# Up projection of a hybrid decoder layer: one PSUM bank per 128-column tile, other uses of the spare banks, and a later place for the query and key transposes

## Chip, cores and metric

The kernel runs on one core of one Trainium2 chip. The metric is device time in microseconds, the median of several executions. The profile is of one execution of the same program.

## The reference

One decoder layer for 256 tokens of width 2048, everything in float32: two attention mixers (8 heads each) on one combined projection, merged by two gates; a squared-ReLU MLP; a gated input embedding.

```python
h = rmsnorm(x, g_mix)
qa, ka, va, qb, kb, vb, ga, gb = split(h @ w_in)              # 2048 x 10240
qa, ka = partial_rope(rmsnorm(qa, qn_gain)), partial_rope(rmsnorm(ka, kn_gain))
ya = dilated_mixture(qa, ka, va)
yb = stick_breaking(qb, kb, vb)
merged = sigmoid(ga) * (ya @ w_branch_a) + sigmoid(gb) * (yb @ w_branch_b)
x = x + merged @ w_out
x = x + square(relu(rmsnorm(x, g_mlp) @ w_up)) @ w_down       # 2048 x 8192, 8192 x 2048
x = x + (p @ w_ple_proj) * sigmoid(rmsnorm(x, g_ple) @ w_ple_gate)
```

## The kernel before

**Number format.** Every weight and activation is split into a high and a low half (`split`, lines 79 to 87: ACT writes the high half on L82, or L85 with a gain; DVE the low half on L83 or L86). A product is three products: high by high, high by low, low by high. A weight load is 1 MB into one of three `raw` buffers (`load`, L91, on SP's queue); `split_weights` cuts it into splits of 1024 columns a row, `wh` and `wl`, three buffers each.

**Order.** The program is written in one order per engine, and a scheduler of the framework, which knows each engine's work and buffers, may draw instructions forward when it lays out the queues. Each engine then works its queue in that order. Steps that should come some time after what they depend on are put off by hand: `later(us, fn)` keeps a step until `advance` has counted that many microseconds of planned matmul time.

**Query and key.** `group_m` (lines 145 to 158) multiplies 16 contraction tiles, 1.3 us of planned time each, into two banks, one for each half of the tokens. `qk_norm` (lines 267 to 288) normalises the heads on ACT and DVE; POOL applies the gain and the rotation (lines 279 to 287). `later(22, qk_transpose, ...)` on L288 puts off four transposes into one bank (L293) and a copy on ACT (L294). The normalised tile `qn` lives in a ring of seven buffers until then.

**MLP.** After the out projection `h2` is made by `turn` (lines 468 to 479): transposes L476 and splits L85, L86, put off by 3 us after each column block. The hidden width of 8192 goes in eight slabs of 1024. `up_units(s)` (lines 555 to 574) makes slab `s` in four groups of two 128-column tiles. A group takes both banks of the tag `mm`; for each of 16 contraction tiles and each column tile `j` there is a pair of matmuls, L565 (512 columns: high weights by both halves of `h2`) and L566 (256 columns: low weights by the high half). `hidden` (lines 529 to 551) then adds the two halves of each bank (ACT copies one on L537, DVE adds on L538, in `hs`), takes relu and square and splits the result `u`.

The down projection of slab `s` runs beside the up projection of slab `s + 1`: `together` interleaves the streams. One column block in two goes by `fast_units`, a seven-product scheme in the four banks of the tag `s`. The other goes by `plain_units` (lines 656 to 676), which takes two banks of the tag `m` for each half block `j`: 48 matmuls on L666 to L668, then two additions into the residual `xr` (L461). The eight banks are thus `mm` 2, `s` 4, `m` 2. The up projection of slab 0 has nothing beside it. The last slab goes by `plain_units` alone, beside the small embedding product. The gate (lines 756 to 768) alternates between `m` and `mm`.

Of the kernel before, what the change touches and what calls it, by code (L numbers as in the profile page):

```python
# [9 lines left out]
F32 = mybir.dt.float32  # L10
F32R = mybir.dt.float32r
AF = mybir.ActivationFunctionType
ALU = mybir.AluOpType
# [3 lines left out]
P = 128  # L17
T = 256
D = 2048
DT = D // P  # L20
# [39 lines left out]
def layer_kernel(ctx: ExitStack, tc: tile.TileContext, xt, xm, pt, gains, qkg, cst,  # L60
                 wa, wb, wba, wbb, wo, wup, wdn, wpg, wpp, out):
    nc = tc.nc
# [43 lines left out]
    def weights(src, nk, cols):  # L106
        return split_weights(load(src, nk, cols), nk, cols)
# [4 lines left out]
    def later(us, fn, *args):  # L112

        pending.append((clock[0] + us, len(pending), fn, args))

    def advance(us):
        clock[0] += us
        while True:
            due = [e for e in pending if e[0] <= clock[0]]
            if not due:  # L120
                return
            e = min(due, key=lambda e: e[:2])
            pending.remove(e)
            e[2](*e[3])

    def flat(a):
        return a.rearrange("p a t -> p (a t)")
# [139 lines left out]
    def qk_norm(ps, tt, g, gain, dst):  # L267
        raw = work.tile([P, 4, DH], F32, tag="w2", name="qraw", bufs=W2)
        sq = work.tile([P, 4, DH], F32, tag="w2", name="qsq", bufs=W2)
        nc.scalar.activation(raw.rearrange("p h d -> p (h d)"), ps, AF.Copy, scale=rt[:, tt:tt + 1])  # L270
        nc.vector.tensor_tensor(sq, raw, raw, op=ALU.mult)
        v = work.tile([P, 4], F32, tag="qv", name="qv")
        r = work.tile([P, 4], F32, tag="qr", name="qr")
        nc.vector.tensor_reduce(v, sq, axis=AX.X, op=ALU.add)
        nc.vector.tensor_scalar(v, v, 1.0 / DH, EPS, op0=ALU.mult, op1=ALU.add)
        rsqrt(r, v, 4)
        qn = work.tile([P, 4, DH], F32, tag="w2", name="qn", bufs=W2)
        nc.vector.tensor_tensor(qn, raw, r[:, :, None].to_broadcast([P, 4, DH]), op=ALU.mult)
        nc.gpsimd.tensor_tensor(qn, qn, gain[:, None, :].to_broadcast([P, 4, DH]), op=ALU.mult)
        ro = work.tile([P, 4, 4, HALF], F32, tag="ro", name="ro", bufs=1)  # L280
        x1, x2 = qn[:, :, :HALF], qn[:, :, HALF:ROT]
        cos = cs[:, C_COS + tt * HALF:C_COS + (tt + 1) * HALF][:, None, :].to_broadcast([P, 4, HALF])
        sin = cs[:, C_SIN + tt * HALF:C_SIN + (tt + 1) * HALF][:, None, :].to_broadcast([P, 4, HALF])
        for n, (a, b) in enumerate(((x1, cos), (x2, sin), (x2, cos), (x1, sin))):
            nc.gpsimd.tensor_tensor(ro[:, n], a, b, op=ALU.mult)
        nc.gpsimd.tensor_tensor(x1, ro[:, 0], ro[:, 1], op=ALU.subtract)
        nc.gpsimd.tensor_tensor(x2, ro[:, 2], ro[:, 3], op=ALU.add)
        later(22, qk_transpose, qn, tt, g, dst)  # L288

    def qk_transpose(qn, tt, g, dst):  # L290
        tp = bank("at")
# [6 lines left out]
    for n, (dst, gain) in enumerate(((qT, gq[:, 0, :]), (kT, gq[:, 1, :]))):  # L298
        for g in range(2):
            if rt is None:  # L300
                ps = group_m(range(4), h, first_weights)
# [4 lines left out]
            else:  # L306
                ps = group_m([wa[2 * n + g, c] for c in range(4)], h)
# [91 lines left out]
    for n, dst in enumerate((qS, kS)):  # L399
        for g in range(4):  # L400
            later(2, dilated_head, 4 * n + g)
            ps = group_t([wb[4 * n + g, c] for c in range(2)], h)
# [17 lines left out]
    for g in range(8):  # L420
        later(2, sb_head, g)
        ps = group_t([wb[8 + g, c] for c in range(2)], h)
        for j in range(2):
            nc.vector.tensor_tensor(gs(2 * g + j), halves(ps[j]), rb, op=ALU.mult)
    for g in range(8):
        ps = group_t([wba[g, 0]], ya)
        for j in range(2):
            k = 2 * g + j
# [4 lines left out]
    m = new_acts("m")  # L433
    for g in range(8):
        pg = group_t([wb[16 + g, c] for c in range(2)], h)
        sg = []
        for j in range(2):
            s = work.tile([P, T], F32, tag="w1", name="sg", bufs=W1)
# [3 lines left out]
        ps = group_t([wbb[g, 0]], yb)  # L442
        for j in range(2):
            k = 2 * g + j
# [52 lines left out]
    h2 = new_acts("h2_", pool=blk)  # L497
    ss1 = const.tile([P, 2, 4], F32, name="ss1")
    for g in range(4):
        ps = group_m([wo[g, c] for c in range(4)], m)  # L500
# [19 lines left out]
    mw = mlp.enter_context(tc.tile_pool(name="mw", bufs=2))  # L520
# [3 lines left out]
    def bank2(tag, bufs=1):  # L524
        return ps2.tile([P, 512], F32, tag=tag, name=f"ps_{tag}", bufs=bufs)

    turn_bank[0] = lambda: bank2("s", 4)

    def hidden(ps, fast):

        n = 8 if fast else 4
        s = mw.tile([P, 2, T], F32, tag="hs", name="hs", bufs=2)
        for j in range(2):
            t = mw.tile([P, T], F32, tag="ev", name="ev", bufs=2)
            nc.scalar.activation(t, ps[j][:, T:], AF.Copy)  # L537
            nc.vector.tensor_tensor(s[:, j, :], ps[j][:, :T], t, op=ALU.add)  # L538
        nc.scalar.activation(s, s, AF.Relu)
        r = mw.tile([P, n, P], F32, tag="hr", name="hr", bufs=1)  # L540
        nc.scalar.activation(r[:, 0:4, :].rearrange("p a t -> p (a t)"),
                             s.rearrange("p a t -> p (a t)"), AF.Square)
        if fast:
            a21, a11, a22, a12 = (r[:, i, :] for i in range(4))
            nc.vector.tensor_tensor(r[:, 4, :], a11, a21, op=ALU.subtract)
            nc.vector.tensor_tensor(r[:, 5, :], a21, a22, op=ALU.subtract)
            nc.vector.tensor_tensor(r[:, 6, :], r[:, 5, :], a11, op=ALU.subtract)
            nc.vector.tensor_tensor(r[:, 7, :], r[:, 6, :], a12, op=ALU.add)
        u = hid.tile([P, 2, n, P], F32R, tag="hid", name="u")
        split(u[:, 0], u[:, 1], r)  # L550
        return u

    A21, A11, A22, A12, S3, S1, S2, S4 = range(8)

    def up_units(s, out):

        for g in range(4):
            ps = [bank2("mm", 2) for _ in range(2)]
            for c in range(2):
                parts = weights(wup[4 * s + g, c], 8, 256)  # L560
                for i, (wh, wl) in enumerate(parts):
                    kt = 8 * c + i
                    for j in range(2):
                        cc = slice(j * P, (j + 1) * P)
                        nc.tensor.matmul(ps[j], wh[:, cc], flat(h2[kt]), start=kt == 0, stop=False)  # L565
                        nc.tensor.matmul(ps[j][:, :T], wl[:, cc], h2[kt][:, 0, :], start=False,  # L566
                                         stop=kt == DT - 1)
                    advance(0.69)
                    if i == 3:
                        yield  # L570
                if c == 0:
                    yield
            out.append(hidden(ps, (s, 0) in FAST or (s, 1) in FAST))
            yield

    def fast_units(s, n, f):

# [78 lines left out]
    def plain_units(s, n, u):  # L656

        for j in range(2):
            ps = [bank2("m", 2) for _ in range(2)]
            for i in range(2):  # L660
                raw = load(wdn[s, n, i, j], 4, PIECE)
                for k, (wh, wl) in enumerate(split_weights(raw, 4, PIECE)):
                    for tt in range(2):
                        a = 2 * i + tt
                        last = i == 1 and k == 3
                        nc.tensor.matmul(ps[tt], u[k][:, 0, a, :], wh, start=i + k == 0, stop=False)  # L666
                        nc.tensor.matmul(ps[tt], u[k][:, 0, a, :], wl, start=False, stop=False)  # L667
                        nc.tensor.matmul(ps[tt], u[k][:, 1, a, :], wh, start=False, stop=last)  # L668
                    advance(1.36)
                    if k == 1:  # L670
                        yield
                if i == 0:
                    yield
            for tt in range(2):
                add_rows(tt, (2 * n + j) * PIECE, ps[tt], r2[:, tt:tt + 1])
            yield
# [52 lines left out]
            finished(2 * n + 1)  # L729

    hids = [[]]
    for _ in up_units(0, hids[0]):
        pass
    for s in range(7):
        hids.append([])
# [18 lines left out]
        nc.sync.dma_start(out[tt, :, c], o)  # L754

    for g in range(4):
        ps = [bank2(("m", "mm")[g % 2], 2) for _ in range(2)]
        for c in range(4):
            for i, (wh, wl) in enumerate(weights(wpg[g, c], 4, PIECE)):
                kt = 4 * c + i  # L760
                for tt in range(2):
                    t = slice(tt * P, (tt + 1) * P)
                    nc.tensor.matmul(ps[tt], h3[kt][:, 0, t], wh, start=kt == 0, stop=False)
                    nc.tensor.matmul(ps[tt], h3[kt][:, 0, t], wl, start=False, stop=False)
                    nc.tensor.matmul(ps[tt], h3[kt][:, 1, t], wh, start=False, stop=kt == DT - 1)
                advance(1.36)
        for tt in range(2):
            gate_out(g, tt, ps[tt], 0, PIECE)
# [3 lines left out]
def tiles_t(w, nk=8):  # L772

    k, n = w.shape
    w = w.reshape(k // (P * nk), nk, P, n // 256, 256).transpose(3, 0, 2, 1, 4)
    return np.ascontiguousarray(w).reshape(n // 256, k // (P * nk), P, nk * 256)
# [9 lines left out]
def tiles_up(w):  # L786

    k, n = w.shape
    w = w.reshape(k, n // 1024, 2, 4, P).transpose(0, 1, 3, 2, 4).reshape(k, n)
    return tiles_t(np.ascontiguousarray(w))  # L790


def quarters(w):
# [50 lines left out]
```

## Time and profile before

| what | us |
|---|---|
| median of 3 runs | 1508.91 (1507.36 to 1509.26) |
| the profiled execution, whole time | 1509.95 |
| its span, first to last instruction | 1508.2 |
| PE busy | 1477.5 (98%) |
| DVE busy | 1067.6 (71%) |
| ACT busy | 857.8 (57%) |
| POOL busy | 57.3 (4%) |

PE runs the matmuls, DVE is the vector engine, ACT the scalar engine, POOL the general engine, SP the queue that issues the loads. The span lies 1.8 us inside the profiled execution's whole time. A matmul's row is longer than its step: its end is modelled and overlaps the next one's start. A wait in brackets at a row is idle time of that engine just before it, and what ended it.

### The profile page before, as it was taken

The page shows a single profiled execution, that of the slowest core. Times are in us where ns is not written, and L with a number is a line of the kernel's source. Part 1 is how long each engine was busy: PE and PEld are TensorE (multiplying, and loading weights), DVE is VectorE, ACT ScalarE, POOL GpSimd, SP SyncE. Part 2 cuts the span into 40 slices and gives each one's busy share as a digit, 9 for nine tenths or more (in the row PEclk, how much of TensorE's full clock was granted, in tenths as well). Part 3 has the DMA queues.
Part 4 walks back from the last instruction along what each step waited for, and adds up shares of the span by engine and source line. Part 5 has one row for each costly group of instructions (what it writes and reads, how often), then busy time and mean ns, then how long its engine had stood idle before and what let it go on. Part 6 is the DMA issues. An engine that isn't in the chain of part 4 may idle for free.

```text
span 1508.2 us, 19034 instructions
## 1 busy us (share of the span) xinstructions
PE 1477.5 (98%) x7412; PEld 1228.9 (81%) x7412; DVE 1067.6 (71%) x1366; ACT 857.8 (57%) x1153; POOL 57.3 (4%) x75
## 2 busy tenths in 40 slices
PE   8999999999999999999999999999999999999998
PEld 5788888888888888888787887878878787878886
DVE  7875666466676676556778879788787878765554
ACT  6454554489845554555555656556565655655543
POOL 3532000000000000000000000000000000000000
PEclk9999999999999999999999999999999999999999
DMA  7555444544455555457355463644636455444563
GB/s 297 206 189 196 168 168 168 187 174 153 161 191 178 185 196 184 179 203 272 122 207 198 153 242 113 246 172 174 217 141 240 149 199 193 157 149 147 198 222 111
DMA packets 40554, 279.16 MB, mean 185 GB/s; under 512 B 4624, under 2 KB 5136, under 8 KB 7312
## 3 DMA queue, kind: packets, MB, share of 16 engines
q1 hardware_dynamic: 40320, 277.92, 51.4%
q8 instruction: 58, 0.95, 0.3%
q14 instruction: 32, 0.26, 0.1%
q10 hardware_dynamic: 144, 0.02, 0.0%
HBM read 275.83 MB, written 2.10 MB: 184 GB/s over the span
## 4 chain that ended last, share of the span: by engine, by line
PE 90%; DVE 5%; ACT 2%; issue 2%; DMA 0%; POOL 0%; SPq 0%; DVEq 0%; ACTq 0%; POOLq 0%
PE ps_mm L138 16%; PE ps_mm L565 15%; PE ps_mm L139 8%; PE ps_mm L566 8%; PE ps_mm L154 5%; PE ps_mm L155 5%; PE ps_mm L153 5%; PE ps_m L667 4%; PE ps_m L668 4%; PE ps_m L666 4%; PE ps_s L584 3%; PE ps_s L586 3%; PE ps_s L588 2%; DVE wl L83 2%; ACT wh L82 2%
## 5 line engine op out<-in xcount | busy, mean ns | idle before, releaser
L83 DVE TENSOR_TENSOR wl<-raw,wh 128x1024 fp32r<-128x1024 f32 (+1 forms) x462 | 566.0, 1231 | 262.5 <-ACT wh L82 257.2
L82 ACT ACTIVATE wh<-raw 128x1024 fp32r<-128x1024 f32 (+1 forms) x462 | 485.4, 1053 | 353.6 <-PE ps_mm L155 112.4
L565 PE MATMUL ps_mm<-h,wh 128*128 128x512 f32 x1024 | 365.9, 399 | 9.1 <-DVE hs L538 6.1
L566 PE MATMUL ps_mm<-h,wl 128*128 128x256 f32 x1024 | 282.9, 281 | 0.6
L138 PE MATMUL ps_mm<-h,wh 128*128 128x512 f32 x768 | 276.8, 403 | 0.0
L565 PEld LDWEIGHTS ps_mm<-h,wh 128*128 128x128 f32 x1024 | 191.4, 188 | 58.8 <-DVE hs L538 11.1
L139 PE MATMUL ps_mm<-h,wl 128*128 128x256 f32 x768 | 215.4, 280 | 0.0
L566 PEld LDWEIGHTS ps_mm<-h,wl 128*128 128x128 f32 x1024 | 192.8, 189 | 9.3 <-DVE wl L83 2.9
L83 DVE TENSOR_TENSOR wl<-quart,wh 128x1024 fp32r<-128x1024 f32 x98 | 119.9, 1224 | 75.4 <-ACT wh L82 74.7
L138 PEld LDWEIGHTS ps_mm<-h,wh 128*128 128x128 f32 x768 | 144.4, 188 | 33.9
L82 ACT ACTIVATE wh<-quart 128x1024 fp32r<-128x1024 f32 x98 | 103.7, 1058 | 95.0 <-PE ps_mm L565 56.8
L139 PEld LDWEIGHTS ps_mm<-h,wl 128*128 128x128 f32 x768 | 145.1, 189 | 0.3
L667 PE MATMUL ps_m<-wl,u 128*128 128x512 f32 x288 | 113.3, 394 | 2.7 <-DVE wl L83 2.7
L666 PE MATMUL ps_m<-wh,u 128*128 128x512 f32 x288 | 111.2, 392 | 2.5 <-DVE xr L461 2.5
L668 PE MATMUL ps_m<-wh,u 128*128 128x512 f32 x288 | 112.5, 391 | 0.0
L153 PE MATMUL ps_mm<-wh,h 128*128 128x512 f32 x256 | 101.4, 399 | 2.7 <-ACT wh L82 2.7
L154 PE MATMUL ps_mm<-wl,h 128*128 128x512 f32 x256 | 101.3, 396 | 2.4 <-DVE wl L83 2.4
L155 PE MATMUL ps_mm<-wh,h 128*128 128x512 f32 x256 | 100.9, 394 | 0.0
L586 PE MATMUL ps_s<-wl,u 128*128 128x512 f32 x196 | 80.3, 410 | 0.0
L584 PE MATMUL ps_s<-wh,u 128*128 128x512 f32 x196 | 79.5, 405 | 0.7 <-ACT wh L82 0.7
L588 PE MATMUL ps_s<-wh,u 128*128 128x512 f32 x196 | 76.7, 392 | 0.0
L667 PEld LDWEIGHTS ps_m<-wl,u 128*128 128x128 f32 x288 | 54.1, 188 | 15.9 <-DVE wl L83 5.3
(210 smaller groups left out, 1989.5 us busy)
## 6 DMA issues: line engine op xcount, KB each, us to landing
raw<-in_wup SPq DMA_DIRECT2D x64, 1024.0 KB, 4.8
raw<-in_wb SPq DMA_DIRECT2D x48, 1024.0 KB, 4.8
raw<-in_wdn SPq DMA_DIRECT2D x36, 1024.0 KB, 4.7
raw<-in_wa SPq DMA_DIRECT2D x31, 1024.0 KB, 4.8
quart<-in_wdn SPq DMA_DIRECT2D x28, 1024.0 KB, 4.7
raw<-in_wo SPq DMA_DIRECT2D x16, 1024.0 KB, 4.8
raw<-in_wpg SPq DMA_DIRECT2D x16, 1024.0 KB, 4.8
raw<-in_wba SPq DMA_DIRECT2D x8, 1024.0 KB, 4.7
```

Source lines behind the costliest of these rows:

```text
L82: nc.scalar.activation(hi, src, AF.Copy)
L83: nc.vector.tensor_tensor(lo, src, hi.bitcast(F32), op=ALU.subtract)
L138: nc.tensor.matmul(ps[j], wh[:, c], flat(rhs[kt]), start=kt == 0, stop=False)
L139: nc.tensor.matmul(ps[j][:, :T], wl[:, c], rhs[kt][:, 0, :], start=False, stop=kt == last)
L153: nc.tensor.matmul(ps[tt], lhs[kt][:, 0, t], wh, start=kt == 0, stop=False)
L154: nc.tensor.matmul(ps[tt], lhs[kt][:, 0, t], wl, start=False, stop=False)
L155: nc.tensor.matmul(ps[tt], lhs[kt][:, 1, t], wh, start=False, stop=kt == last)
L565: nc.tensor.matmul(ps[j], wh[:, cc], flat(h2[kt]), start=kt == 0, stop=False)
L566: nc.tensor.matmul(ps[j][:, :T], wl[:, cc], h2[kt][:, 0, :], start=False, stop=kt == DT - 1)
L666: nc.tensor.matmul(ps[tt], u[k][:, 0, a, :], wh, start=i + k == 0, stop=False)
L667: nc.tensor.matmul(ps[tt], u[k][:, 0, a, :], wl, start=False, stop=False)
L668: nc.tensor.matmul(ps[tt], u[k][:, 1, a, :], wh, start=False, stop=last)
```

## The change

1. `up_units` goes through the two tiles of a group one after the other. Each tile takes one bank, loads its own 1 MB (16 contraction tiles of 128 columns; the host lays `w_up` out for that) and is added up (ACT copy, DVE addition) at its own end. `hidden` gets the sums. The planned time of a pair is counted singly.
2. Slab 0 takes its banks from the tag `s` (four banks) in place of `mm`.
3. In the last slab the second half of each block takes two banks of `s` in place of `m`.
4. The gate alternates between `s` and `m`.
5. The query and key transposes are emitted 32 us of planned time after their group, not 22.

```diff
-        later(22, qk_transpose, qn, tt, g, dst)
+        later(32, qk_transpose, qn, tt, g, dst)
...
-    def hidden(ps, fast):
+    def hidden(s, fast):
         n = 8 if fast else 4
-        s = mw.tile([P, 2, T], F32, tag="hs", name="hs", bufs=2)
-        for j in range(2):
-            t = mw.tile([P, T], F32, tag="ev", name="ev", bufs=2)
-            nc.scalar.activation(t, ps[j][:, T:], AF.Copy)
-            nc.vector.tensor_tensor(s[:, j, :], ps[j][:, :T], t, op=ALU.add)
         nc.scalar.activation(s, s, AF.Relu)
...
-    def up_units(s, out):
+    def up_units(s, out, tag="mm"):
         for g in range(4):
-            ps = [bank2("mm", 2) for _ in range(2)]
-            for c in range(2):
-                parts = weights(wup[4 * s + g, c], 8, 256)
-                for i, (wh, wl) in enumerate(parts):
-                    kt = 8 * c + i
-                    for j in range(2):
-                        cc = slice(j * P, (j + 1) * P)
-                        nc.tensor.matmul(ps[j], wh[:, cc], flat(h2[kt]), start=kt == 0, stop=False)
-                        nc.tensor.matmul(ps[j][:, :T], wl[:, cc], h2[kt][:, 0, :], start=False,
-                                         stop=kt == DT - 1)
-                    advance(0.69)
-                    if i == 3:
+            sums = mw.tile([P, 2, T], F32, tag="hs", name="hs", bufs=2)
+            for j in range(2):
+                ps = bank2(tag, 4 if tag == "s" else 2)
+                parts = split_weights(load(wup[4 * s + g, j], DT, P), DT, P)
+                for kt, (wh, wl) in enumerate(parts):
+                    nc.tensor.matmul(ps, wh, flat(h2[kt]), start=kt == 0, stop=False)
+                    nc.tensor.matmul(ps[:, :T], wl, h2[kt][:, 0, :], start=False, stop=kt == DT - 1)
+                    advance(0.347)
+                    if kt == 7:
                         yield
-                if c == 0:
-                    yield
-            out.append(hidden(ps, (s, 0) in FAST or (s, 1) in FAST))
-            yield
+                t = mw.tile([P, T], F32, tag="ev", name="ev", bufs=2)
+                nc.scalar.activation(t, ps[:, T:], AF.Copy)
+                nc.vector.tensor_tensor(sums[:, j, :], ps[:, :T], t, op=ALU.add)
+                if j == 1:
+                    out.append(hidden(sums, (s, 0) in FAST or (s, 1) in FAST))
+                yield
...
         for j in range(2):
-            ps = [bank2("m", 2) for _ in range(2)]
+            ps = [bank2("s", 4) if j and s == 7 else bank2("m", 2) for _ in range(2)]
...
-    for _ in up_units(0, hids[0]):
+    for _ in up_units(0, hids[0], "s"):
...
-        ps = [bank2(("m", "mm")[g % 2], 2) for _ in range(2)]
+        ps = [bank2("m", 2) if g % 2 else bank2("s", 4) for _ in range(2)]
```

## Rows read from the trace of the kernel before

**Rows 1.** The page: busy time of each engine; engines in the chain that ended last.
```profile
PE 1477.5 (98%) x7412; PEld 1228.9 (81%) x7412; DVE 1067.6 (71%) x1366; ACT 857.8 (57%) x1153; POOL 57.3 (4%) x75
...
PE 90%; DVE 5%; ACT 2%; issue 2%; DMA 0%; POOL 0%; SPq 0%; DVEq 0%; ACTq 0%; POOLq 0%
```

**Rows 2.** Waits of PE: who waited for whom, total us, times, longest.
```profile
PE ps_mm L565 <- DVE hs L538: 6.1, 11, 0.6
...
PE ps_at L293 <- POOL qn L287: 2.7, 1, 2.7
PE ps_m L667 <- DVE wl L83: 2.7, 6, 0.5
PE ps_m L666 <- DVE xr L461: 2.5, 3, 1.6
...
PE ps_mm L565 <- DVE xr L459: 1.0, 1, 1.0
```

**Rows 3.** Timeline, end of slab 0: start, duration, engine, operation [idle before <- releaser].
```profile
723.12 0.38 ACT L537 ACTIVATE ev<-ps_mm 128x256 f32<-128x256 f32 x1 [1.53 <-PE ps_mm L566]
723.15 0.28 PE L566 MATMUL ps_mm<-h,wl 128*128 128x256 f32 x1
...
723.53 0.42 DVE L538 TENSOR_TENSOR hs<-ps_mm,ev 128x256 f32<-128x256 f32 x1 [0.69 <-ACT ev L537]
...
724.01 0.50 PE L565 MATMUL ps_mm<-h,wh 128*128 128x512 f32 x1 [0.58 <-DVE hs L538]
...
724.35 0.28 PE L566 MATMUL ps_mm<-h,wl 128*128 128x256 f32 x1
...
724.46 0.39 PE L565 MATMUL ps_mm<-h,wh 128*128 128x512 f32 x1
...
724.69 0.28 PE L566 MATMUL ps_mm<-h,wl 128*128 128x256 f32 x1
...
725.62 0.42 DVE L538 TENSOR_TENSOR hs<-ps_mm,ev 128x256 f32<-128x256 f32 x1
```

**Rows 4.** Timeline of PE: first and last of the ten like waits.
```profile
687.80 0.50 PE L565 MATMUL ps_mm<-h,wh 128*128 128x512 f32 x1 [0.58 <-DVE hs L538]
...
1288.82 0.51 PE L565 MATMUL ps_mm<-h,wh 128*128 128x512 f32 x1 [0.57 <-DVE hs L538]
```

**Rows 5.** Timeline, slab 0: transposes of the last column block and its low halves.
```profile
678.55 1.04 PE L476 MATMUL ps_s<-idt,xr 128*128 128x128 f32 x8
...
680.56 0.87 DVE L86 SCALAR_TENSOR_TENSOR h<-ps_s,gn,h 128x256 fp32r<-128x256 f32 x2
...
681.59 0.88 DVE L86 SCALAR_TENSOR_TENSOR h<-ps_s,gn,h 128x256 fp32r<-128x256 f32 x2
```

**Rows 6.** Timeline of PE in the last slab: two waits of the down projection.
```profile
1369.42 0.47 PE L666 MATMUL ps_m<-wh,u 128*128 128x512 f32 x1 [0.45 <-DVE xr L461]
1369.73 0.39 PE L667 MATMUL ps_m<-wl,u 128*128 128x512 f32 x1
...
1399.48 0.47 PE L666 MATMUL ps_m<-wh,u 128*128 128x512 f32 x1 [0.50 <-DVE xr L461]
```

**Rows 7.** Timeline, first query group: transposes on PE, POOL's last instruction before them.
```profile
58.26 0.60 PE L293 MATMUL ps_at<-idt,qn 128*128 128x128 f32 x4
61.56 0.66 PE L293 MATMUL ps_at<-idt,qn 128*128 128x128 f32 x4 [2.71 <-POOL qn L287]
...
61.20 0.31 POOL L287 TENSOR_TENSOR qn<-ro 128x64 f32<-128x64 f32 x1
```

**Rows 8.** Windows: stretch, length, busy time by engine, granted clock, DMA share, GB/s.
```profile
62.00:66.80 4.80, 4.80 (x17) 3.80 (x15) 3.11 (x7) 2.32 (x4) 1.90 (x2) 0.64 0.13 53
```

**Rows 9.** Timeline of DVE beside POOL's work, first query group.
```profile
49.18 1.79 DVE L271 TENSOR_TENSOR qsq<-qraw 128x512 f32<-128x512 f32 x1
...
55.02 3.46 DVE L83 TENSOR_TENSOR wl<-raw,wh 128x1024 fp32r<-128x1024 f32 x2
...
59.84 1.22 DVE L83 TENSOR_TENSOR wl<-raw,wh 128x1024 fp32r<-128x1024 f32 x1
```

More of the change, by code (lines that the diff above doesn't have):

```diff
@@ L788, in tiles_up @@
     k, n = w.shape
-    w = w.reshape(k, n // 1024, 2, 4, P).transpose(0, 1, 3, 2, 4).reshape(k, n)
-    return tiles_t(np.ascontiguousarray(w))
+    w = w.reshape(k // P, P, n // 1024, 2, 4, P).transpose(2, 4, 3, 1, 0, 5)
+    return np.ascontiguousarray(w).reshape(n // 256, 2, P, k)
 def quarters(w):
```

## The prediction

> **What bounds the kernel now.** I read the page first, then the waits of the matmul engine, then the timeline around the longest of these waits, then the busy time by stage. The page shows PE busy for 98% of the span and PE with 90% of the chain that ended last [rows 1]. So only two things can move the time: matmul work, and the moments in which PE stands still. The change removes no matmul, so all that can be won lies in those moments. The waits view names them [rows 2]: 6.1 us in 11 waits of the up projection for the addition that empties its banks (L565 on L538), one wait of 2.7 us of a transpose for POOL (L293 on L287), 2.5 us in 3 waits of the down projection (L666 on L461), 2.7 us in 6 waits for a low half of the weights (L667 on L83), and one of 1.0 us at the start of the up projection (L565 on L459).
>
> These figures are too small, because a matmul's row ends after its successor could have started. I measure losses from start to start. At 723.15 PE starts the last matmul of a group and at 724.01 the first of the next; the usual step between these two forms is 724.35 to 724.46. So 0.86 less 0.11 is 0.75 us lost, of which the view counts 0.58. The next step takes 0.34 (724.01 to 724.35) where 0.23 is usual (724.46 to 724.69), another 0.11 [rows 3]. One such wait costs 0.85 us.
>
> **Up projection, tile by tile.** Before, a group fills both mm banks at once and ends in both within 0.35 us, so the next group has no bank. Its first matmul waits for a copy on ACT (723.12) and an addition on DVE (723.53, ended 723.95) [rows 3]. There are ten of these with the same 0.57 to 0.59 us of idle time: four in the first slab, where nothing else fills the gap, and one in each of six later slabs; the first and the last stand in [rows 4]. Ten times 0.85 is 8.5 us. The eleventh wait is another 0.28 us of idle time; I leave its 0.4 us to the lower end of the range. After the change a tile takes one bank for 16 pairs of matmuls. At a pair of 0.34 to 0.35 us (724.35 to 724.69) [rows 3] that is 5.6 us, and the other bank must be emptied in that time, for which copy and addition now need 0.8 us from 723.12 to 723.95. In the first slab the tiles go round four banks, so there is more room still. All 8.5 us go.
>
> What is next? The work beside it is of the same amount: 64 copies, 64 additions, 64 loads of 1 MB, splits of 1024 columns a row, each still feeding 16 matmuls. These cost nothing as long as they run beside PE. But they move: ACT and DVE now meet a copy at each tile's end, not two per group. A copy at the head of ACT's queue holds back the weight split behind it, and the addition on DVE holds back the low half behind that. This is the first rival.
>
> Is it dearer to accumulate many times running into one bank? Before, pairs alternate banks by the program. But just after the wait at 724.01 the second bank is still full (its addition ends at 726.04), so the pairs there all go into one bank, and their steps are 0.11 and 0.23 us, as elsewhere [rows 3]. I cost it at nothing.
>
> **The last column block of h2.** Its transposes are emitted 3 us of planned time after the out projection. Before, that is after ten pairs, and h2[12] is used from pair 25 on. Now it comes after nine pairs and h2[12] is the thirteenth. So PE has three pairs, 1.04 us, and the eight transposes, 0.9 us, between the first transpose and the first use: 1.9 us, and 3.0 us to h2[15]. In the trace the first transpose starts at 678.55 and the two pairs of low halves end at 681.43 and 682.47: 2.9 us for h2[13], 3.9 us for h2[15] [rows 5]. That is a new wait of up to 0.9 us, plus 0.1 for the slow step after it. It is nothing if PE takes the next tile's matmuls first (order of execution is not order of emission: after 724.01 four pairs of one bank run before the other bank's). Between 0 and 1.0 I take 1.0, since the rows give it. The 1.0 us wait for L459 ahead of it [rows 2] is the first use of the new set of banks after the old one; that remains.
>
> **The last slab.** It has no up projection beside it, so each half block waits for the two additions of the one before. Two of the three waits on L461 are inside it, at 1369.42 and 1399.48, with 0.45 and 0.50 us idle [rows 6]. With 0.16 for the matmul's tail and 0.08 for the step after (1369.42 to 1369.73 is 0.31) each costs about 0.7 us. The second half now has banks of its own, and each m bank then gets a whole half block (48 matmuls, 11 us) to be emptied: 1.4 us go. The third, the longest of that row at 1.6 us [rows 2], stands at the slab's start, where j is 0 and the m banks are still used. It stays. For the gate the banks were alternated before as well, and no wait of L763 is in the view: nothing.
>
> **Query and key transposes.** The four transposes at 58.26 run; the next four wait until 61.56 for POOL's last instruction of that head group (61.20, ended 61.51) [rows 7]. Four transposes take 0.44 us, so 2.86 us are lost. Then the clock: over the next 4.8 us the granted clock is 0.64 [rows 8], between its two levels of 1.2 and 2.4 GHz, after PE had stood for those 2.9 us. At 0.64 those 4.8 us lose 0.36 of themselves, 1.7 us. Emitting them 10 us later puts them near 69 us, 7 us after POOL is done: 4.6 us go. What is moved are transposes and their copies on ACT; no DMA. The normalised rows hold their buffer longer, two tiles of a ring of seven, with at most five others alive: no wait there.
>
> Does something take the place of this wait? DVE is the engine to look at. Beside POOL its instructions are slow: 1.79 us at 49.18, and two splits in 3.46 us at 55.02, against 1.22 us at 59.84 [rows 9]. A split feeds twelve matmuls, and at 58.26 PE is six into one (22 us of planned time end one contraction tile after the next group's start). If it goes on at once, at 0.23 us a matmul it wants the next low half seven steps on, at 59.9; that one ended at 58.48. The one after it is wanted 2.7 us later, at 62.6, and ended at 61.06. So 1.4 and 1.5 us are in hand, and it holds. The Trainium skill says in "SBUF — State Buffer", section "Who interferes with whom", that a VectorE instruction with two SBUF inputs contends with a GpSimd instruction that reads SBUF. The slow rows agree with this. By it, this part would give back some of its gain (second rival).
>
> **Sum.** 8.5 + 1.4 + 4.6 - 1.0 = 13.5 us. The profiled execution took 1509.95 us, so 1496.4; the median of the runs shown lies 1.0 us below it, so **1495.4 us**. The unknown is the order in which the steady slabs' splits come out. They hold one wait for a low half each, six in all [rows 2], worth about 0.7 us start to start; whether these vanish or double is open: 4 to 5 us each way.
>
> **Rivals.**
> First, slower: the copies starve PE of weights. Place: the 56 tile ends of the later seven slabs. Price: 0.7 us for each at which the split behind the copy comes late. It decides from 19 tile ends on (13.5 by 0.7), one in three. At half of them, 28, it costs 19.6 us: 1515 us. For it: ACT sat idle 1.53 us ahead of the copy at 723.12 [rows 3]. Against it: with the same ring of three split buffers PE waits for low halves only 2.7 us in all [rows 2]. Chance 0.10.
>
> Second, a part is given back: behind the transposes DVE, slowed by POOL, becomes the limit and returns some 2.5 of the 4.6 us, and the slabs' splits fall worse by their 4.5. 1495.4 + 7 = 1502 us. Chance 0.14, a third of it close enough to the old time to look like no change.
>
> Third, the change does not do what it says: the scheduler draws the tile after next forward and it waits for its bank as before. The 8.5 us stay: 1504 us. Against it: 5.6 us per tile to empty a bank in 0.8. Chance 0.06, half of it as no change.
>
> Fourth, better: the six waits for low halves go too and the h2 wait is covered: 1495.4 - 4.5 - 1.0 = 1490 us. Chance 0.08.
>
> **How the numbers follow.** The forecast has 0.62. The range from 1490 to 1505 holds it, half of the fourth case and most of the second and third: 0.62 + 0.04 + 0.13 + 0.04 is 0.83. A difference under 0.2% (3.0 us) can't be told from no change here. Faster: 0.62 + 0.08 + 0.09 + 0.03 = 0.82. Same: 0.05 + 0.03 = 0.08. Slower: 0.10.
>
> **What would show it.** In the waits of PE: no row of the up projection waiting for its bank's addition; L293 not waiting for POOL; L666 waiting once, for 1.6 us, and not three times. In the windows: granted clock of 1.00 through 58 to 70 us. The first slab shorter by about 2.4 us net (four waits gone, the h2 wait new). Wrong would be: PE waiting in the slabs for L83 or L82 by more than 5 us beyond before, or lost steps of more than 0.12 between pairs in the same bank.

## The result and the profile of the changed kernel

The changed kernel takes 1493.02 us (median of four, 1492.89 to 1493.25). The kernel before, run beside it on the same chip, takes 1508.57 us (median of four, 1507.36 to 1509.26). The ratio is 0.9895, with a 95% interval from 0.9883 to 0.9907: 15.6 us less. The prediction said 1495.4 us, in a range from 1490 to 1505.

The first view is again the page's: the span, the busy time of each engine, and the engines in the chain that ended last. It answers [rows 1].

```profile
span 1491.4 us, 19033 instructions
...
PE 1474.4 (99%) x7412; PEld 1229.8 (82%) x7412; DVE 1064.7 (71%) x1366; ACT 856.4 (57%) x1153; POOL 59.2 (4%) x75
...
PE 93%; DVE 3%; issue 2%; ACT 1%; DMA 0%; SPq 0%; DVEq 0%; ACTq 0%
```

The matmuls are the same 7412, and DVE and ACT run as many instructions in almost the same time. PE's share of the chain went from 90% to 93%: PE stands still less. The waits of PE (who waited for whom, total us, times, longest) show which of them went. They answer [rows 2]; in the new code the up projection's pair is L558 and L559, and the plain down projection is L660 to L662.

```profile
PE ps_m L661 <- DVE wl L83: 3.9, 7, 1.2
PE ps_mm L153 <- ACT wh L82: 2.0, 2, 1.0
PE ps_m L660 <- DVE xr L461: 1.6, 1, 1.6
PE ps_at L195 <- DVE warm L193: 1.5, 1, 1.5
PE ps_s L558 <- DVE xr L459: 1.0, 1, 1.0
PE ps_mm L154 <- DVE wl L83: 0.6, 1, 0.6
```

All eleven waits for the addition into `hs` are gone, the wait of the transposes for POOL is gone, and of three waits for the residual (L461) one is left, the one of 1.6 us. The six waits for a low half are now seven. Around the query and key transposes the windows answer [rows 8] (stretch, length, busy time of PE, PEld, DVE, ACT and POOL, granted clock, DMA share, GB/s):

```profile
58.20:62.00 3.80, 3.80 (x18) 3.18 (x17) 3.33 (x9) 1.23 (x3) 2.71 (x5) 1.00 0.73 261
62.00:66.80 4.80, 4.80 (x22) 3.95 (x22) 4.75 (x5) 1.45 (x2) 3.88 (x5) 1.00 0.42 131
```

PE is busy for all of both stretches and the clock stays at 1.00, that is 2.4 GHz.

To see where the time went I take the first matmul of each stage in both traces and subtract. The second measured column is another profiled execution of the same changed kernel; it tells how far one execution may be trusted.

| stage | forecast, us saved | measured | a second execution |
|---|---|---|---|
| start to the first query group's end | 0 | 0.5 | 0.3 |
| query and key | 4.6 | 4.5 | 4.4 |
| value, gates, out projection | 0 | -0.2 | -0.2 |
| slab 0 of the up projection | 3.4 - 1.0 = 2.4 | 2.8 | 3.5 |
| slab 1 | 0 | 2.4 | 2.2 |
| slabs 2 to 7 | 6 x 0.85 = 5.1 | 5.0 | 4.3 |
| last slab and gate | 1.4 | 1.9 | 1.9 |
| sum | 13.5 | 16.7 | 16.4 |

The entries are rounded one by one. The forecast's terms are there, each in its stage. Most of the surplus stands in slab 1, where the sum had nothing.

### The profile page after: what moved, and what is told of

Its sections match the earlier page's. It is cut to its first block, busy times and chain, and to the rows that moved or that the text cites. A ratio compares the mean times of both kernels' runs of the same rounds, so it can differ in the third digit from the quotient of the medians.

```text
span 1491.4 us, 19033 instructions
## 1 busy us (share of the span) xinstructions
PE 1474.4 (99%) x7412; PEld 1229.8 (82%) x7412; DVE 1064.7 (71%) x1366; ACT 856.4 (57%) x1153; POOL 59.2 (4%) x75
## 4 chain that ended last, share of the span: by engine, by line
PE 93%; DVE 3%; issue 2%; ACT 1%; DMA 0%; SPq 0%; DVEq 0%; ACTq 0%
PE ps_mm L138 16%; PE ps_mm L558 13%; PE ps_mm L139 8%; PE ps_mm L559 7%; PE ps_mm L154 6%; PE ps_mm L155 6%; PE ps_mm L153 6%; PE ps_m L661 4%; PE ps_m L662 4%; PE ps_m L660 3%; PE ps_s L580 3%; PE ps_s L578 2%; PE ps_s L582 2%; PE ps_s L558 2%; DVE wl L83 2%
## 5 line engine op out<-in xcount | busy, mean ns | idle before, releaser
L558 PE MATMUL ps_mm<-h,wh 128*128 128x512 f32 x896 | 320.4, 397 | 0.0
L138 PE MATMUL ps_mm<-h,wh 128*128 128x512 f32 x768 | 277.0, 403 | 0.0
L559 PE MATMUL ps_mm<-h,wl 128*128 128x256 f32 x896 | 251.6, 281 | 0.4
L139 PE MATMUL ps_mm<-h,wl 128*128 128x256 f32 x768 | 215.5, 281 | 0.0
L558 PEld LDWEIGHTS ps_mm<-h,wh 128*128 128x128 f32 x896 | 168.2, 188 | 40.3 <-ACT wh L82 2.3
L559 PEld LDWEIGHTS ps_mm<-h,wl 128*128 128x128 f32 x896 | 168.9, 189 | 7.9 <-DVE wl L83 3.2
L138 PEld LDWEIGHTS ps_mm<-h,wh 128*128 128x128 f32 x768 | 144.4, 188 | 34.0
L139 PEld LDWEIGHTS ps_mm<-h,wl 128*128 128x128 f32 x768 | 145.1, 189 | 0.3
L661 PE MATMUL ps_m<-wl,u 128*128 128x512 f32 x256 | 101.9, 398 | 4.0 <-DVE wl L83 3.9
L662 PE MATMUL ps_m<-wh,u 128*128 128x512 f32 x256 | 100.2, 391 | 0.0
L660 PE MATMUL ps_m<-wh,u 128*128 128x512 f32 x256 | 97.9, 392 | 1.6 <-DVE xr L461 1.6
L592 DVE TENSOR_TENSOR quart<-quart 128x2048 f32<-128x2048 f32 x28 | 64.0, 2287 | 0.5
```

Source lines behind the costliest of these rows:

```text
L138: nc.tensor.matmul(ps[j], wh[:, c], flat(rhs[kt]), start=kt == 0, stop=False)
L139: nc.tensor.matmul(ps[j][:, :T], wl[:, c], rhs[kt][:, 0, :], start=False, stop=kt == last)
L558: nc.tensor.matmul(ps, wh, flat(h2[kt]), start=kt == 0, stop=False)
L559: nc.tensor.matmul(ps[:, :T], wl, h2[kt][:, 0, :], start=False, stop=kt == DT - 1)
```

## The experiments

Each kernel is compared with the kernel before on the same chip; the edits to the changed kernel also with the changed kernel itself, on its chip. The first theory is the prediction's: the parts add up, each by the standstill of PE that it removes. The rivals are that the ends of the tiles starve PE of weights, that DVE beside POOL gives a part back, and that the spare banks, not the tiles, bring the gain.

**The transposes alone.**

```diff
-        later(22, qk_transpose, qn, tt, g, dst)
+        later(32, qk_transpose, qn, tt, g, dst)
```

> The kernel before with the query and key transposes emitted 32 us of planned time after their group, nothing else changed. Theory (the wait for POOL costs its 2.9 us and the clock drop behind it 1.7 us): 4.6 us faster than before, 1504.0 us, and a granted clock of 1.00 through 58 to 70 us. Rival (DVE, slowed by POOL, takes over and gives back about 2.5 us): 2 us faster, 1506.5 us, with waits of PE for low halves of the weights between 60 and 80 us.

Measured: 1505.33 us against 1509.97, ratio 0.9971 (0.9959 to 0.9982), 4.6 us less. The windows of this run, with the same columns as above:

```profile
58.20:62.00 3.80, 3.80 (x19) 3.14 (x17) 3.46 (x7) 0.73 (x3) 3.34 (x6) 1.00 0.59 196
62.00:66.80 4.80, 4.80 (x23) 3.98 (x22) 4.63 (x8) 2.08 (x3) 3.25 (x4) 1.00 0.39 123
```

The standstill and the lower clock are both gone, and DVE, though slow beside POOL, gives nothing back. The second rival falls here.

**The tiles alone**, in the `mm` banks in every slab; transposes, last slab and gate as before.

```diff
+    def up_units(s, out, tag="mm"):
...
+            for j in range(2):
+                ps = bank2(tag, 4 if tag == "s" else 2)
...
     for _ in up_units(0, hids[0]):
```

> The kernel before with the up projection tile by tile, one bank each, in the two mm banks in every slab; transposes at 22, last slab and gate as before. Theory (each of ten waits for an emptied bank costs 0.85 us start to start, and the tiles remove all of them): 8.5 us faster, less at most 0.2 us for the last column block of h2, 1500 us. As the trace of the changed kernel has some 2 us fewer lost in slab 1 than the sum had, up to 10.5 us faster, 1498 us, if that belongs to the tiles. Rival (the first slab needs the four s banks): waits of L558 for the addition remain in slab 0, and it is 5 to 6 us faster, 1503 us.

Measured: 1499.83 us, ratio 0.9934 (0.9922 to 0.9947), 10.1 us less. Three lines of its waits of PE:

```profile
PE ps_m L661 <- DVE wl L83: 4.0, 7, 1.2
PE ps_at L293 <- POOL qn L287: 2.7, 1, 2.7
...
PE ps_m L660 <- DVE xr L461: 2.5, 3, 1.5
```

No wait for `hs` is left, and the waits that belong to the other parts of the change stand as before. So two banks are enough in slab 0 as well, and the prediction's third rival (the scheduler draws a tile forward that then waits for its bank) falls. The tiles by themselves bring 10.1, more than the 8.5 less 1.0 of the sum. By stage it is 3.5 us in slab 0, 2.0 in slab 1 and 3.9 in slabs 2 to 7.

**The last slab alone.**

```diff
-            ps = [bank2("m", 2) for _ in range(2)]
+            ps = [bank2("s", 4) if j and s == 7 else bank2("m", 2) for _ in range(2)]
```

> The kernel before with the second half of each block of the last slab in two s banks, nothing else changed. Theory (two waits of 0.7 us each go): 1.4 us faster, 1507.2 us. Rival (the additions are only put off and meet the next half or the transposes for the gate): no change, 1508.6 us, with a new wait of PE between 1369 and 1415 us.

Measured: 1507.79 us, ratio 0.9987 (0.9978 to 0.9996), 2.2 us less; its trace shows 2.1 us of this between the start of the last slab and the gate. The same trace has something else in it:

```profile
PE ps_at L293 <- POOL qn L287: 2.7, 1, 2.7
...
62.00:66.80 4.80, 4.80 (x23) 3.94 (x21) 3.80 (x8) 2.97 (x5) 2.25 (x1) 1.00 0.12 46
```

PE stood for the same 2.7 us as before, and the clock did not fall: 1.00 where [rows 8] has 0.64. The same standstill can come without the lower clock behind it. So a median of these runs may hold some of the clock too, and the 2.1 us of the stage are the better figure for the last slab.

**The whole change with the transposes at their old place.**

```diff
-        later(32, qk_transpose, qn, tt, g, dst)
+        later(22, qk_transpose, qn, tt, g, dst)
```

> The changed kernel with the transposes put back to 22 us. Theory (the parts add up, none covers another): it is slower than the changed kernel by the same 4.6 us as the first run is faster than before, 1497.6 us. Rival (the later stages have slack that hides part of it, or a shift of the stages costs something elsewhere): a difference that is off by more than 1.5 us from that.

Measured: 1498.4 us, ratio 0.9919 (0.9906 to 0.9933), 11.6 us less. Its window:

```profile
62.00:66.80 4.80, 4.80 (x17) 3.89 (x18) 2.39 (x7) 2.33 (x4) 1.60 (x2) 0.64 0.21 85
```

Wait and lower clock are both back. The other parts are worth 11.6 us together. Against the changed kernel, which ran on other chips (1493.02 and 1493.58 us), this is 4.8 to 5.4 us slower where the theory said 4.6, so nothing here speaks for the rival.

**The changed kernel once more, with two edits to it.** The changed kernel itself comes first, as the standard for the edits to it that ran on the same chip:

> The changed kernel itself, beside the next runs on one chip. If the three parts add up, it is faster than before by the sum of the first three runs, 4.6 + 10.1 + 2.2 = 17 us; if the parts cover each other, by clearly less.

Measured: 1493.58 us against 1508.91, ratio 0.99 (0.9885 to 0.9915). That is 15.3 us, less than the 17 of the expectation; what this says of the sum stands with the transposes in the next section. Then slab 0 in two banks, not four:

```diff
-    for _ in up_units(0, hids[0], "s"):
+    for _ in up_units(0, hids[0]):
```

> The changed kernel with slab 0 in the two mm banks in place of the four s banks. Theory (a tile's 5.6 us cover the 0.8 us in which the other bank is emptied, so two banks are enough): no change against the changed kernel, within 0.5 us. Rival (the spare banks do the work in slab 0): waits of L558 for the addition come back there, 0.85 us for each tile end, up to 6 us slower.

Measured: 1493.58 us, the same median. With tiles, two banks are enough: a tile's bank is emptied while the next tile is multiplied, and the spare banks in slab 0 bring nothing.

Then twice the work at a tile's end on ACT:

```diff
                 nc.scalar.activation(t, ps[:, T:], AF.Copy)
+                nc.scalar.activation(t, ps[:, T:], AF.Copy)
                 nc.vector.tensor_tensor(sums[:, j, :], ps[:, :T], t, op=ALU.add)
```

> The changed kernel with each tile's copy on ACT done twice: 64 more copies of 0.3 to 0.4 us, 24 us of ACT time. Theory (ACT and DVE have room, and a copy at a tile's end does not hold back the splits that PE needs next): less than 1 us slower than the changed kernel. Rival (the copies at the head of ACT's queue starve PE of weights): half of the tile ends cost 0.3 us or more, 10 us slower, with more waits of PE for L82 and L83.

Measured: 1493.36 us, ratio 0.9898 (0.9883 to 0.9913). 64 more copies of some 0.4 us on ACT cost nothing that can be seen, and the waits in the slabs stay as they were (the lines of this kernel stand one further down):

```profile
PE ps_m L662 <- DVE wl L83: 4.0, 7, 1.2
...
PE ps_mm L154 <- DVE wl L83: 0.9, 1, 0.9
```

So the copy at the head of ACT's queue does not starve PE. The first rival falls.

**Two banks more instead of tiles.** The kernel before, its groups of two tiles unchanged, with slab 0 in the `s` banks:

```diff
-            ps = [bank2("mm", 2) for _ in range(2)]
+            ps = [bank2("mm", 2) if s else bank2("s", 4) for _ in range(2)]
```

> The kernel before with only the banks of slab 0 changed: its groups of two tiles take two of the four s banks in turn, the order of the matmuls stays that of groups. Theory (it is the free bank that wins, not the order of the tiles): the three waits inside slab 0 and the one at its end go, 3.4 us faster than before, 1505.5 us; the six waits of later slabs stay. Rival (the tile order itself is needed, for instance since copies of both banks at once hold back the splits): less than 1.5 us faster, with other waits of PE in slab 0. Slab 1, where the tiles lost 2 us less than the sum had: if that comes with slab 0 running through, it shows here too; if it comes with the order of the tiles, slab 1 is as before.

Measured: 1507.2 us against 1508.97, ratio 0.9992 (0.9983 to 1.0001): 1.8 us less, about half of what the four waits of slab 0 cost, and the interval reaches 1. It is neither the theory's 3.4 nor the rival's less than 1.5, so the trace has to tell. There slab 0 takes 45.4 us against 49.0 before, 3.6 shorter, and slab 1 takes 93.3 against 91.5, 1.8 longer. Three of PE's six idle times in slab 1 (start, duration, engine, operation [idle before <- releaser]):

```profile
730.23 0.50 PE L667 MATMUL ps_m<-wl,u 128*128 128x512 f32 x1 [1.21 <-DVE wl L83]
...
745.05 0.50 PE L586 MATMUL ps_s<-wl,u 128*128 128x512 f32 x1 [0.76 <-DVE wl L83]
...
747.92 0.50 PE L565 MATMUL ps_mm<-h,wh 128*128 128x512 f32 x1 [1.21 <-DVE hs L538]
```

The gain in slab 0 was given back in part one slab later, as waits for splits and as a bank wait of twice the usual size. The tiles do not give it back: with them slab 0 takes 45.5 us (46.3 in the first trace of the changed kernel), and slab 1 takes 89.1 to 89.5.

**The transposes one contraction tile later.** This leaves a standstill of half the length:

```diff
-        later(22, qk_transpose, qn, tt, g, dst)
+        later(22.8, qk_transpose, qn, tt, g, dst)
```

> The kernel before with the query and key transposes emitted one contraction tile (1.36 us) later than before. Theory (the clock drop is set off by the length of the standstill): PE waits 1.5 us for POOL in place of 2.9 us, the clock stays at 1.00 in every execution, and it is 1.4 us faster, or up to 3.1 us where the kernel before had the drop; its executions lie within 1 us of each other. Rival (a standstill of 1.5 us also drops the clock in some executions): a granted clock under 1.00 after 62 us, and executions that lie 1.7 us apart, 1.4 us faster on the whole.

Measured: 1505.98 us against 1508.97, ratio 0.9982 (0.9973 to 0.999), 3.0 us less. Its wait and its windows:

```profile
PE ps_at L293 <- POOL qn L287: 1.3, 1, 1.3
...
58.20:62.00 3.80, 2.47 (x16) 1.95 (x15) 3.39 (x9) 0.87 (x2) 3.07 (x6) 1.00 0.66 231
62.00:66.80 4.80, 4.80 (x23) 3.96 (x22) 4.66 (x7) 2.90 (x5) 3.51 (x5) 1.00 0.39 118
```

PE waits 1.3 us by the view (1.5 from start to start), and the clock stays at 1.00. The theory held: 3.0 us lies in its 1.4 to 3.1. Eleven executions of this kernel lie within 0.8 us (1505.51 to 1506.3); 21 of the kernel before, on the same chip, spread over 3.2 us (1507.24 to 1510.41). That the clock held in all eleven is read from how close they lie; one of them has a trace.

**A version that beats both.** In the changed kernel two waits on the residual are left, the one of 1.6 us at the start of the last slab and the one of 1.0 at the start of the up projection. The first needs banks other than `m` for the first half block too. The second was the first use of a new set of banks, so here the banks of the mixers are kept throughout (`bank2` gives `at` for `s`, `mm` for the rest).

```diff
-    psum = mixers.enter_context(tc.tile_pool(name="psum", bufs=4, space=PSUM))
+    psum = ctx.enter_context(tc.tile_pool(name="psum", bufs=4, space=PSUM))
...
-        return ps2.tile([P, 512], F32, tag=tag, name=f"ps_{tag}", bufs=bufs)
+        return bank("at" if tag == "s" else "mm")
...
-            ps = [bank2("s", 4) if j and s == 7 else bank2("m", 2) for _ in range(2)]
+            ps = [bank2("s", 4) if s == 7 and (j or n == 0) else bank2("m", 2) for _ in range(2)]
```

> A version beyond the changed kernel: the first half of the last slab's first block also takes two s banks, and the MLP keeps the PSUM pool of the mixers (s in its four at banks, m and mm in its four mm banks) in place of a new pool. Theory (two waits are left that banks can remove: 1.7 us at the start of the last slab for L461, 1.1 us at the start of the up projection for L459): 2.8 us faster than the changed kernel. Rival (with m and mm in one ring of four the tiles and half blocks wait for each other): slower than the changed kernel, with waits of L558 or L660 for additions in every slab.

Measured: 1490.67 us against 1493.58 of the changed kernel on the same chip; ratio to the kernel before 0.9879 (0.9863 to 0.9896). All its waits of PE (the lines of this kernel stand one further up):

```profile
PE ps_mm L660 <- DVE wl L83: 3.8, 7, 1.2
PE ps_mm L154 <- DVE wl L83: 2.1, 2, 1.4
PE ps_mm L153 <- ACT wh L82: 2.0, 2, 1.2
PE ps_at L195 <- DVE warm L193: 1.5, 1, 1.5
```

Both waits on the residual are gone, and the time falls by 2.9 us.

## Why the prediction was right, and where its sum was off

**The bound.** It held: the saving is PE's standstills. Counted from start to start over the usual step of each form (0.227 us at 512 columns, 0.117 at 256), in the steps that are over it by more than 0.02 us, PE loses 60.4 us in the trace of before and 43.4 after. Both kernels run the same matmuls, so these 17.0 us had to come near the difference of the spans, 16.8; they show that no usual step became dearer.

**The ten bank waits, 8.5 us.** Right in place and size. In slab 0 either means would do: tiles in two banks and groups in four take the same time there. But the groups in four banks lose half of it again in slab 1, and in the later slabs, where the down projection uses the `s` banks, the tiles remove the waits with two. A long run into one bank costs nothing, as forecast. In the trace of before, between the start of a group and the addition that empties its second bank, where only one bank can be written, the step from L566 to L565 has a mean of 117 ns, as elsewhere; in the changed kernel's slab 0, where a tile has one bank, it is 117 ns too.

**Slab 1, mis-sized: 0 in the sum, 2.2 to 2.4 measured.** I listed the waits by total and left those under the first rows aside. Four lines of PE's timeline of before, in slab 1, would have shown what lies there:

```profile
734.75 0.73 PE L565 MATMUL ps_mm<-h,wh 128*128 128x512 f32 x2 [1.39 <-ACT wh L82]
...
749.38 0.51 PE L565 MATMUL ps_mm<-h,wh 128*128 128x512 f32 x1 [0.28 <-DVE hs L538]
...
750.61 0.50 PE L584 MATMUL ps_s<-wh,u 128*128 128x512 f32 x1 [0.73 <-ACT wh L82]
...
759.90 0.73 PE L565 MATMUL ps_mm<-h,wh 128*128 128x512 f32 x2 [0.67 <-ACT wh L82]
```

Together they are 3.1 us of idle time, 3.85 from start to start, in the first slab that has a down projection beside it. The changed kernel has one long wait left there:

```profile
726.11 0.50 PE L661 MATMUL ps_m<-wl,u 128*128 128x512 f32 x1 [1.22 <-DVE wl L83]
```

With a small one of 0.07 at 763.76 it costs 1.6 us from start to start, so 2.2 are saved. But for the 0.28, the eleventh bank wait, these are waits for splits, and the change does not lessen the splits; it changes the order in which the queues hold them. The prediction left such an order open for the six low-half waits, "4 to 5 us each way"; the waits for high halves in slab 1 were in none of its terms. The tiles alone show 2.0 us too, so neither the later transposes nor the last slab's banks are needed for it. Whether it is the order of the loads and splits (one load now serves one tile, where two served the two tiles of a group) or the place of the copies that does it, no run tells.

**The wait for the last block of h2, mis-sized: 1.0 us in the sum, some 0.2 measured.** I took the upper end, and the lower was right. After the transposes (begun at 673.48) the timeline shows:

```profile
675.83 0.87 DVE L86 SCALAR_TENSOR_TENSOR h<-ps_s,gn,h 128x256 fp32r<-128x256 f32 x2
...
676.08 0.78 PE L558 MATMUL ps_s<-h,wh 128*128 128x512 f32 x2
...
676.70 0.40 PE L559 MATMUL ps_s<-h,wl 128*128 128x256 f32 x2
676.85 0.88 DVE L86 SCALAR_TENSOR_TENSOR h<-ps_s,gn,h 128x256 fp32r<-128x256 f32 x2
```

PE runs on through the low halves of DVE; the two steps that are late lose 0.05 and 0.11 us. The way out that the prediction named did come. Nine pairs ran before the transposes, so three of this tile were left ahead of `h2[12]`, whose low half DVE ended at 676.31. But PE starts six pairs from 674.27 to 676.08, so three of them can only be of the next tile. What failed is the choice of 1.0 between 0 and 1.0: the rows gave the wait for pairs in the order in which they are written, and they did not run in that order.

**The last slab, 1.4 us in the sum, 1.9 to 2.1 measured.** Both waits inside it went. Two smaller ones that no bracket marks went too: in the trace of before transposes stand ahead of the first use of a bank and hide most of the wait.

```profile
1383.14 0.60 PE L476 MATMUL ps_s<-idt,xr 128*128 128x128 f32 x4
1383.75 0.47 PE L666 MATMUL ps_m<-wh,u 128*128 128x512 f32 x1
1384.05 0.39 PE L667 MATMUL ps_m<-wl,u 128*128 128x512 f32 x1
```

Four transposes take 0.44 us, so L666 is 0.17 late, and the step after it takes 0.30 instead of 0.23: 0.25 us, and as much at 1413.79. The 1.6 us at the slab's start stayed, as forecast.

**The transposes, 4.6 us.** Right for the profiled execution (4.4 to 4.5 in the stage). For the median it is 2.9 us of standstill and, in some executions only, 1.7 us of clock; the trace with 2.7 us of wait and a clock of 1.00 speaks for this. It also bears on whether the parts add up. The medians of the three parts give 4.6 + 10.1 + 2.2 = 16.9 us and the whole change 15.3 to 15.6, but the parts ran on another chip, on which the kernel before took 1.0 to 1.4 us longer in the median. In the traces, stage by stage, the parts save 4.5 + 9.4 + 2.1 = 16.0 us, and the changed kernel 16.5 and 16.3 in the same stages: they add up to within 0.5. I had set the profiled execution 1.0 us above the median without asking why; the clock is the likely reason, though no run takes the two apart for one execution. It also made the forecast look better than its sum: from one profiled execution to the other the saving is 16.7 us, 3.2 more than the 13.5, and from median to median 2.1 more. The 1.1 us between the two are luck.

**The second rival came close.** For the two nearest low halves the room was 1.4 and 1.5 us, as worked out. I stopped there. POOL worked on, and the next ones had 0.9, 0.09 and 0.5 us in hand. The narrowest ended its split at 67.40, and the matmul that uses it starts on time at 67.49, though its step takes 0.30 us instead of 0.23 (the low half on DVE, then the matmul):

```profile
66.18 1.22 DVE L83 TENSOR_TENSOR wl<-raw,wh 128x1024 fp32r<-128x1024 f32 x1
...
67.49 0.46 PE L154 MATMUL ps_mm<-wl,h 128*128 128x512 f32 x1
```

A little less room and the term would have shrunk. The Trainium skill says in "SBUF — State Buffer", section "Who interferes with whom", that a VectorE instruction with two SBUF inputs contends with a GpSimd instruction that reads SBUF. The slow rows of before agree (1.79 us at 49.18); that a part of the gain would be given back did not follow, as the windows with PE busy throughout show.

One row was misread there. The split at 59.84, which took 1.22 us and stood for DVE without POOL, ran beside POOL too. In that place POOL was the slow one (trace of before):

```profile
53.08 0.32 POOL L286 TENSOR_TENSOR qn<-ro 128x64 f32<-128x64 f32 x1
...
60.01 1.22 POOL L286 TENSOR_TENSOR qn<-ro 128x64 f32<-128x64 f32 x1
```

The same instruction took 0.9 us more, and it ended 0.2 us after the split did. So some 0.9 us of PE's standstill, by an estimate from these two rows, came from DVE holding back POOL; no run moves that split to test it.

**The six low-half waits in the slabs** stayed at like places, one a slab from slab 2 on, and cost 0.7 us each from start to start, as forecast. Neither the fourth rival's end nor its opposite came.

## What to carry to other kernels

When one engine bounds a kernel, count its lost steps from start to start by stage, small ones and ones without a bracket too, before summing the named waits. A wait for a bank is removed by filling banks one after the other so that one empties while the next fills; more banks for the same order may only move the wait into the next stage. Where an engine is slowed for a while, work out the room of every entry up to the end of that while: the narrowest need not be among the first.

## What the runs showed of the hardware that I had not expected

The same standstill of PE lowered its clock in some executions and not in others. With about 2.7 us of wait the granted clock of the next 4.8 us was 0.64 in four traces (the kernel before, the tiles alone, the whole change with the old place, the groups in spare banks) and 1.00 in a fifth (the last slab alone). With 1.3 us it was 1.00 in the one trace, and the eleven executions lay within 0.8 us. In the four traces the clock fell only after PE had resumed, and not at one moment: with the groups in spare banks PE resumed at 61.57 and the granted clock from 62.0 to 62.5 was 0.53, while in the kernel before PE resumed at 61.56 and that clock was still 1.00, and 0.50 from 63.0 on. The Trainium skill, "TensorE: Matmul & The Clock Gate", section "Part 1: The HAM clock gate", says that what the chip counts activity by runs free of the kernel's start, so that the moment of a clock change varies between runs; these traces agree.

A lower clock need not cost time. In the changed kernel's own trace the granted clock is 0.57 from 16 to 20 us, and in its run with slab 0 in two banks 1.00. Yet the second query group starts at 34.4 us in the one and at 34.7 in the other: early on PE waits for weights, and in the trace with the lower clock a wait of 1.4 us at 23 us is missing.
